# A decoder step on one core: the first two units run side by side on inputs that come in pieces of 256 KB, with zeros multiplied before and between

## The chip, the cores and the metric

The kernel runs on 1 core of one Trainium2 chip. The time is that of one execution on the device in microseconds (us); lower is better. Before the change the median of 3 runs is 2367.28 us (2366.43 to 2371.67).

## What is computed

One inference step of a decoder with two layers: 1024 prompt tokens and 8 single decode tokens, model width 2048, all in float32. Layer A mixes by pooling, layer B by attention over a sliding window:

```python
z = x @ w_in                               # 2048 -> 4096
u, gate = z[..., :D_POOL], z[..., D_POOL:]
d, new_state = multiscale_pool(u, prefix, pos)        # windows 2, 4, 8, 16 on four channel groups
d = jnp.einsum('btgc,gce->btge', d.reshape(B, T, 4, 512), w_grp)
y = (d.reshape(B, T, D_POOL) * scale * jax.nn.silu(gate)) @ w_out
x = layer_norm(ALPHA * x + y, g_ln, b_ln)
```

Then keys and values are projected once, and layer B does its query and gate projection, attention, output projection and norm. The change lies in the first 2% of the time: in `z = x @ w_in` for the first of the four channel groups.

## The kernel before

**Numbers in two parts.** A float32 operand is split into a high part (rounded to the matmul's type fp32r by a cast on ScalarE) and a low part (operand minus high part, on VectorE). A product is then three matmuls: high x high, high x low, low x high. So each weight block and each block of x costs one cast and one subtraction before its first full use.

**Units.** The tokens are cut in two chunks. The first stage, layer A's input projection of chunk 0 for channel group 0, is done plainly; later stages use a scheme with seven products for eight, whose operands are sums made on the way. A plain unit (`unit`, L648 on) makes 128 output channels for 512 tokens in one PSUM bank: two halves (`par`), each with one weight block (128 x 1024 numbers, 512 KB) and four blocks of x (each two of the 128-channel slices, 512 KB), eight slices of three matmuls (L669, L670, L671), 48 matmuls of 512 columns in all. The group has four such units for u, then four for the gate, and then the group's own product (`group_half`, L1071). Two neighbouring units use the same blocks of x, so x is split once and kept.

**The order of the work.** All of it is written out by Python in one order, and `in_order` keeps that order on TensorE, VectorE and ScalarE. A stream lists the weight blocks in the order of use. `begin` loads ahead (5 blocks), casts ahead (4) and makes low parts ahead (3) in plain stages, then hands out the next pair of high and low parts; `prep_to` (L489) emits the low parts, `cast_to` (L474) the casts, `load_to` (L273) the loads on SP. `end` closes a half of a half unit: it counts `i` up, runs the events due at `i`, and emits one of the sums that wait in `late`. `flush` emits what waits for a finished PSUM bank.

For the plain stage the four blocks of two neighbouring weight tiles (a and d of the first, b and c of the second) are also summed in four ways (`plain_pair`, `add1`, L279) and stored to DRAM by POOL for the second chunk; these sums are the `late` ones. `t_first` (L719 to L722) makes four blocks of sums from two blocks of x for the next stage, at events 3, 6, 9 and 12. A finished unit is copied from PSUM by ScalarE (L1132) and pooled on VectorE (`pool_tile`, L1017, L1025, L1028) at an event one step later.

**The start** (`start`, L2048 on). SP loads weight block a, four blocks of x, block d, two of x, block b, two of x, the small tables prm, cst, mki, and goes on with weights (c first). Eight DMAs of SP's queue can be under way: the ninth waits for the first, and so on. ScalarE casts and VectorE subtracts whole blocks (128 x 1024) in the order a, x 0 to 3, d, x 4 to 7; then nsink (L2077), a small scaling of a part of prm. Memory is 53 slots of 128 x 1040 numbers; a new tile takes the slot that has been free longest.

Of the kernel before, what the change touches and what calls it, by code (L numbers as in the profile page):

```python
# [16 lines left out]
P = 128  # L17
# [13 lines left out]
TP = 512  # L31
# [30 lines left out]
ORDERL = (0, 5, 2, 1, 3, 4, 6)  # L62
ENGINES = (mybir.EngineType.PE, mybir.EngineType.DVE, mybir.EngineType.Activation)
NSLOT = 53
KEEP0 = 1

SPLIT = 5, 6, 7
# [114 lines left out]
class Kern:  # L182
    def __init__(self, ctx, tc, io):
# [18 lines left out]
        self.sgd = [one.tile([P, 8, NDEC], F32, name=f"sgd{i}") for i in range(2)]  # L202
        self.mem = Mem(pool("mem", bufs=1), NSLOT)
        self.n = 0
# [62 lines left out]
        u, v = w[2 * q], w[2 * q + 1]  # L267
        return u[:, :1024], u[:, 1024:], v[:, :1024], v[:, 1024:]

    def load1(self, s, k, src):  # L270
        def go():
            s[k] = self.mem.full()
            self.nc.sync.dma_start(s[k].a[:, :1024], src)  # L273

        return go

# [9 lines left out]
    def plain_pair(self, name, q):  # L286

        a11, a12, a21, a22 = self.quads(name, q)
        ws = self.ws[name][q]
        s = {}  # L290
        ent = lambda k, src, after: Entry([self.load1(s, k, src)], [], lambda: s[k], after)
        late = [
            self.add1(s, "c", "b", "c", ws[:, 1, :]),
            self.add1(s, "b", "a", "b", ws[:, 0, :], "b"),
            self.add1(s, "a", "a", "c", ws[:, 2, :], "c"),
            self.add1(s, "d", "a", "d", ws[:, 3, :], "a", "d"),
        ]
        return [
            ent("a", a11, []),
            ent("d", a12, []),  # L300
            ent("b", a21, []),
            ent("c", a22, [lambda: self.late.extend(late)]),
        ]

    def lone(self, src):
        s = {}
        return Entry([self.load1(s, "a", src)], [], lambda: s["a"], [lambda: s.pop("a").free()])
# [347 lines left out]
    def unit(self, done):  # L655
# [3 lines left out]
        for par in range(2):  # L659
            w = self.begin()  # L660
            wh, wl = (s.r for s in w)
            for k in range(8):
# [16 lines left out]
                if k in (3, 7):  # L679
                    self.end()  # L680


    def x_begin(self, n):

        kind, c, part = PHASES[n]
        self.ready((INPUT_OF[kind], c, PHASES[n] in PLAIN))
        self.xkey, self.need = (INPUT_OF[kind], c), {}
        self.xseven = PHASES[n] not in PLAIN
        order = ORDERL if (kind, c) in LOCKED else ORDER7
        self.xq = [(i, g) for i in order for g in range(2)] if self.xseven else [  # L690
            (q, j) for q in range(2) for j in range(4)
        ]
        self.xraw, self.pre = self.pre, {}
        self.held = set(self.xraw)
        self.xhi, self.xnew = {}, {}
        if PHASES[n - 1] in PLAIN and PHASES[n - 1][:2] == (kind, c):

            T = CHUNKS[c][1]
            left = {s: 2 for j in range(4) for s in self.X[1, j]}
            self.shared = True  # L700
            for g in range(2):
                tiles = list(zip(self.X[1, 2 * g], self.X[1, 2 * g + 1]))
                for i, cs in ((5, slice(0, T // 2)), (4, slice(T // 2, T))):
                    self.xnew[i, g] = tuple(View(t, T, cs, left) for t in tiles)
            self.xq = [k for k in self.xq if k not in self.xnew]
        self.xl = [k for k in self.xq if k not in self.held]
# [408 lines left out]
    def phase_ai(self, c, gs, nxt):  # L1115
        nc, io = self.nc, self.io
        T = CHUNKS[c][1]
        TH = T // 2
        silu = lambda dst, ps: nc.scalar.activation(dst, ps, AF.Silu)
        for g in gs:  # L1120
            ext = es = None
            if T > TP:
                es = self.mem.half()
                ext = es.a[:, :512].rearrange("p (i b w) -> p i b w", i=4, b=NDEC)
                nc.sync.dma_start(ext, io["st"][:, 4 * g : 4 * g + 4])
            dd, sg = {}, {}
            for i in range(4):
                if not self.strassen:

                    def done(ps, i=i):  # L1130
                        U = self.mem.full()
                        nc.scalar.copy(U.a[:, NST : NST + T], ps[:])  # L1132
                        self.at(1, lambda: self.pool_tile(c, 4 * g + i, U, None, dd))

                    self.unit(done)
                elif i % 2 == 0:
                    us = {}

                    def z(j, us=us):
                        def go():  # L1140
                            us[j] = self.mem.full()
                            return us[j].a[:, NST : NST + T]

                        return go

                    def done(i=i, us=us):
                        n = i // 2
                        self.at(n, lambda: self.pool_tile(c, 4 * g + i, us[0], ext, dd))
                        self.at(n + 4, lambda: self.pool_tile(c, 4 * g + i + 1, us[1], ext, dd))

                    self.pair(c, z(0), z(1), done)
            if ext is not None:

                def put(es=es, ext=ext, g=g):
                    nc.sync.dma_start(io["nps"][:, 4 * g : 4 * g + 4], ext)
                    es.free()

                self.at(8, put)
            for i in range(4):
                if g == gs[-1] and i == 0:  # L1160
                    self.x_begin(nxt)
                if not self.strassen:

                    def done(ps, i=i):
                        if i % 2 == 0:
                            sg[i // 2] = self.mem.full()
                        silu(sg[i // 2].a[:, (i % 2) * T : (i % 2 + 1) * T], ps[:])

                    self.last = g == gs[-1] and i == 3
                    self.unit(done)  # L1170
                elif i % 2 == 0:
# [78 lines left out]
    def shifted(self, c, p, s, pre, acc, end):  # L1250
# [10 lines left out]
        def less():  # L1261
            t = self.pair_view(s, T)
            nc.vector.tensor_sub(t, t, self.l_sh[c].a[:, None, :T].to_broadcast([P, 2, T]))
            if p >= KEEP0:
                nc.gpsimd.dma_start(self.act["p", c][:, 2 * p : 2 * p + 2, :], t)
# [5 lines left out]
        def add():  # L1271
# [4 lines left out]
            box["q"].free()  # L1276
            if p >= KEEP0:
                s.free(True)
# [774 lines left out]
    def start(self):  # L2053
        nc, io = self.nc, self.io
        self.xkey, self.xseven = ("x", 0), False
        self.X, self.xnew, self.xraw, self.xhi = {}, {}, {}, {}
        self.xq = [(q, j) for q in range(2) for j in range(4)]
        self.xl = list(self.xq)
        self.x0, self.pre, self.held = {}, {}, set()
        self.load_to(1)  # L2060
        for n in range(8):
            self.x_load()
            if n in (3, 5):
                self.load_to(n // 2 + 1)
        nc.sync.dma_start(self.prm[:], io["prm"])
        nc.sync.dma_start(self.cst[:], io["cst"])
        nc.sync.dma_start(self.mki[:], io["mki"])
        self.prep_to(1)
        for n in range(8):
            self.x_make()  # L2070
            if n == 3:
                self.prep_to(2)
        for j in range(4):
            self.at(3 + 3 * j, lambda j=j: self.t_first(j))
        self.at(13, lambda: setattr(self, "x0", None))
        self.at(9, lambda: nc.scalar.copy(self.jr[:], self.cst[:, K_J : K_J + P]))
        nc.vector.tensor_scalar(  # L2077
            self.nsink[:], self.prm[:, C_SINK : C_SINK + NH], -1.0, None, op0=ALU.mult
        )
# [231 lines left out]
```

## Time and profile before

| what | value |
|---|---|
| median of 3 runs | 2367.28 us (2366.43 to 2371.67) |
| the profiled execution | 2367.62 us |
| its span (first to last instruction) | 2365.9 us |
| mean granted clock of TensorE | 0.996 |
| VectorE, ScalarE, POOL busy | 81%, 57%, 9% |
| data moved by DMA | 669.18 MB, 283 GB/s on average |
| DMA, 0 to 8 us, 8 to 13.3 us, 13.3 to 22 us | 242, 407, 399 GB/s |
| DMA, 34 to 100 us | 214 GB/s |

How to read it: the profile is of one execution. PE is TensorE's matmul, PEld its weight loads, DVE is VectorE, ACT ScalarE, POOL GpSimd, SP the engine that issues loads. A row of the timeline has the start in us, the duration in us, engine, line, operation, the tile written and the tile read (m is any of the memory slots, pD a PSUM bank), shapes, count, and in brackets the idle time before it with what ended it. A row of waits has who waited for whom, the sum in us, the number of times and the longest. A row of windows has, behind the stretch, its length, then busy us and count for PE, PEld, DVE, ACT and POOL, then the granted clock, the DMA engines' share and GB/s. A row of groups has busy us and mean ns of one behind the bar. Matmuls are pipelined: the start of one to the start of the next is what one costs, not its duration.

### The profile page before, as it was taken

Reading aid. Unit: us, or ns where it says so; the run is one execution under the profiler, and the core shown is the slowest. Engines: PE = TensorE matmul, PEld = TensorE weight load, DVE = VectorE, ACT = ScalarE, POOL = GpSimd, SP = SyncE. Lnnn points to the kernel's source line nnn. Section 1 sums busy time; section 2 is a strip of 40 time slices with the busy share of each in tenths; the row PEclk is TensorE's granted clock in tenths of the full one; section 3 lists DMA queues with packets and bytes.
Section 4 is the critical chain, followed back from the end, with each engine's and each line's share of the span. In section 5 each row is a group of like instructions: output and inputs, shape, how many; then the busy total and the mean of one; then the engine's idle time right before and its main releaser. Section 6 shows DMA issues by size and latency. Waiting matters only on the chain. (4 is left out here: it accounts for less than half of the span.)

```text
span 2365.9 us, 46542 instructions
## 1 busy us (share of the span) xinstructions
PE 2326.4 (98%) x18424; PEld 2219.4 (94%) x18424; DVE 1923.5 (81%) x2385; ACT 1342.2 (57%) x2429; POOL 201.5 (9%) x379
## 2 busy tenths in 40 slices
PE   8999999999999999999999999999999999999997
PEld 6899999999999999998778899999999999999997
DVE  8787998776878878868888888887777768888887
ACT  4444446544536547554554656685666667546556
POOL 0111110001000000000111111100000000000000
PEclk9999999999999999999999999999999999999999
DMA  8678789889889989989888766788787768699785
GB/s 294 215 244 303 274 291 349 308 308 315 286 278 365 331 270 324 334 314 330 282 324 322 258 230 224 238 297 275 232 259 221 222 193 298 227 353 371 259 302 194
DMA packets 252059, 669.18 MB, mean 283 GB/s; under 512 B 25760, under 2 KB 106560, under 8 KB 251840
## 3 DMA queue, kind: packets, MB, share of 16 engines
q1 hardware_dynamic: 206368, 501.14, 64.0%
q0 software_dynamic: 45472, 165.07, 17.9%
q8 instruction: 144, 2.36, 0.4%
q14 instruction: 75, 0.61, 0.1%
HBM read 471.01 MB, written 185.59 MB: 278 GB/s over the span
## 5 line engine op out<-in xcount | busy, mean ns | idle before, releaser
L641 PE MATMUL pD<-m,m 128*128 128x260 f32 (+1 forms) x4752 | 1346.9, 283 | 9.9 <-DVE m L602 3.7
L643 PE MATMUL pD<-m,m 128*128 128x260 f32 (+1 forms) x4752 | 1340.5, 282 | 4.5 <-DVE m L489 4.5
L642 PE MATMUL pD<-m,m 128*128 128x260 f32 (+1 forms) x4752 | 1340.3, 282 | 0.0
L641 PEld LDWEIGHTS pD<-m,m 128*128 128x128 f32 x4752 | 896.0, 189 | 21.0 <-issue 10.2
L643 PEld LDWEIGHTS pD<-m,m 128*128 128x128 f32 x4752 | 896.7, 189 | 6.0 <-DVE m L489 6.0
L642 PEld LDWEIGHTS pD<-m,m 128*128 128x128 f32 x4752 | 896.3, 189 | 0.5
L489 DVE TENSOR_TENSOR m<-m,m 128x1024 fp32r<-128x1024 f32 x674 | 814.1, 1219 | 96.1 <-ACT m L474 58.3
L474 ACT CAST m<-m 128x1024 fp32r<-128x1024 f32 x674 | 701.6, 1048 | 305.2 <-DVE m L332 71.3
L669 PE MATMUL pD<-m,m 128*128 128x512 f32 x448 | 179.7, 401 | 8.0 <-ACT m L752 8.0
L670 PE MATMUL pD<-m,m 128*128 128x512 f32 x448 | 177.2, 396 | 0.5 <-DVE m L761 0.5
L671 PE MATMUL pD<-m,m 128*128 128x512 f32 x448 | 177.2, 396 | 0.0
L761 DVE TENSOR_TENSOR m<-m,m 128x1024 fp32r<-128x1024 f32 (+1 forms) x120 | 146.9, 1225 | 7.2 <-ACT m L752 5.7
L614 ACT COPY m<-pD 128x260 f32<-128x260 f32 (+1 forms) x83 | 31.0, 373 | 188.2 <-PE pD L643 188.1
L752 ACT CAST m<-m 128x1024 fp32r<-128x1024 f32 (+1 forms) x120 | 125.7, 1052 | 14.2 <-PE pD L670 5.2
L669 PEld LDWEIGHTS pD<-m,m 128*128 128x128 f32 x448 | 84.7, 189 | 29.9 <-ACT m L752 8.0
L332 DVE TENSOR_TENSOR m<-m,m 128x1024 f32<-128x1024 f32 x88 | 107.6, 1222 | 5.9 <-DMA m<-in_wia 4.2
L670 PEld LDWEIGHTS pD<-m,m 128*128 128x128 f32 x448 | 84.8, 189 | 20.4 <-DVE m L761 1.6
L671 PEld LDWEIGHTS pD<-m,m 128*128 128x128 f32 x448 | 84.6, 189 | 19.8
L602 DVE TENSOR_TENSOR m<-pD,m 128x260 f32<-128x260 f32 (+1 forms) x86 | 36.4, 424 | 81.9 <-PE pD L643 78.6
L1778 ACT ACTIVATE m<-m,sm 128x128 f32<-128x128 f32 x256 | 99.2, 390 | 0.0
L1071 PE MATMUL pD<-m,m 128*128 128x260 f32 (+1 forms) x528 | 91.5, 323 | 0.0
L607 DVE TENSOR_TENSOR m<-pD,m 128x260 f32<-128x260 f32 (+1 forms) x84 | 35.6, 424 | 64.2 <-PE pD L643 64.0
(243 smaller groups left out, 2167.3 us busy)
## 6 DMA issues: line engine op xcount, KB each, us to landing
m<-in_wia SPq DMA_DIRECT2D x124, 512.0 KB
m<-in_wib SPq DMA_DIRECT2D x120, 512.0 KB
swia<-m POOLq DMA_DIRECT2D x64, 512.0 KB, 4.9
m<-swia SPq DMA_DIRECT2D x64, 512.0 KB
m<-swoa SPq DMA_DIRECT2D x64, 512.0 KB
swib<-m POOLq DMA_DIRECT2D x64, 512.0 KB, 5.3
m<-swib SPq DMA_DIRECT2D x64, 512.0 KB
m<-swob SPq DMA_DIRECT2D x56, 512.0 KB
```

The lines of the kernel that those rows point to most:

```text
L332: self.nc.vector.tensor_add(s[out].a[:, :1024], s[x].a[:, :1024], s[y].a[:, :1024])
L474: self.nc.scalar.copy(hi.r[:, :1024], self.stream[self.cast].src().a[:, :1024])
L489: self.nc.vector.tensor_sub(lo.r[:, :1024], s.src().a[:, :1024], hi.a[:, :1024])
L641: nc.tensor.matmul(ps[:, :TH], wh[:, s], h, start=new and k == 0, stop=False, skip_group_check=on)
L642: nc.tensor.matmul(ps[:, :TH], wh[:, s], l, start=False, stop=False, skip_group_check=on)
L643: nc.tensor.matmul(ps[:, :TH], wl[:, s], h, start=False, stop=k == 7, skip_group_check=on)
L669: nc.tensor.matmul(ps[:], wh[:, s], h, start=par == 0 and k == 0, stop=False)
L670: nc.tensor.matmul(ps[:], wh[:, s], l, start=False, stop=False)
L671: nc.tensor.matmul(ps[:], wl[:, s], h, start=False, stop=par == 1 and k == 7)
L752: self.nc.scalar.copy(h.r[:, :n], s.a[:, :n])
L761: self.nc.vector.tensor_sub(l.r[:, :n], s.a[:, :n], h.a[:, :n])
L1778: nc.scalar.activation(x["s3"][:, i, :], x["s3"][:, i, :], AF.Exp, bias=nm[:, i : i + 1], scale=0.125, accum_out=rs[:, i : i + 1],)
```

## The change

The first two units run side by side. `first_units` takes the place of the first two calls of `unit`: for each block of x it does six matmuls of the first unit and then six of the second, into two PSUM banks. The first pair's stream is a, b, d, c instead of a, d, b, c.

`start` loads the first half (512 columns, 256 KB) of a, both slices of x block 0 apart (256 KB each), the first half of b, both slices of x block 1, the second half of a, x block 2, the second half of b, x block 3, then d, x 4, c, x 5, x 6, x 7, one weight block more, and prm, cst, mki. Casts and subtractions follow the same pieces, in the same order.

A tile of zeros is made by VectorE, and 17 matmuls of it (256 columns, into a bank of its own) come before the first real one; four stand behind the first real matmul, one in the second slice, and one behind each of the first three groups of six.

Both finished units are handed to ScalarE together; the pooling of the second comes at an event three steps later instead of one. In the built program, VectorE's order behind the last subtraction of x is now nsink, four sums (add1), four operations of t_first, the low part of the third unit's first weights; before it was nsink, the low parts of b and c, two sums, t_first, that low part, and then the other two sums. After the third unit's start TensorE's instructions are the same, in the same order, in both programs; the slots that tiles get differ.

```diff
+WARM = 17
+FILL = 4, 1, 1, 1, 1
...
-        return [
+        e = [
             ent("a", a11, []),
             ent("d", a12, []),
             ent("b", a21, []),
             ent("c", a22, [lambda: self.late.extend(late)]),
         ]
+        return [e[0], e[2], e[1], e[3]] if first else e
...
+    def idle(self, n):
+        z = self.zero
+        for _ in range(n):
+            self.nc.tensor.matmul(self.zps[:, :256], z.r[:, :P], z.r[:, P:384], start=True, stop=True)
+
+    def first_units(self, dones):
+        nc = self.nc
+        banks = [self.psD() for _ in dones]
+        for par in range(2):
+            ws = {}
+            for n, (u, j) in enumerate((u, j) for j in range(4) for u in range(2)):
+                if u not in ws:
+                    ws[u] = self.begin()
+                elif n % 2 == 0:
+                    self.flush()
+                wh, wl = (a.r for a in ws[u])
+                x = self.x_get((par, j))
+                for i in range(2):
+                    k = 2 * j + i
+                    s = slice(k * P, (k + 1) * P)
+                    h, l = (a.rv(2, TP)[:, i, :] for a in x)
+                    nc.tensor.matmul(banks[u][:], wh[:, s], h, start=par == 0 and k == 0, stop=False)
+                    if par == 0 and n == 0:
+                        self.idle(FILL[i])
+                    nc.tensor.matmul(banks[u][:], wh[:, s], l, start=False, stop=False)
+                    nc.tensor.matmul(banks[u][:], wl[:, s], h, start=False, stop=par == 1 and k == 7)
+                if par == 0 and n < 3:
+                    self.idle(FILL[2 + n])
...
+                        n = 3 if g == 0 and i == 1 else 1
+                        self.at(n, lambda: self.pool_tile(c, 4 * g + i, U, None, dd))
+                    if c == 0 and g == 0 and i < 2:
+                        twins.append(done)
+                        if i == 1:
+                            self.first_units(twins)
+                    else:
+                        self.unit(done)
...
-        self.load_to(1)
-        for n in range(8):
+        z = self.zero = self.mem.full()
+        nc.vector.memset(z.a[:, :384], 0.0)
+        self.zps = self.psD()
+        self.idle(WARM)
...
+        plan = [
+            ("a", 0, 512), ("x", 0, TP), ("x", TP, 2 * TP), ("b", 0, 512), ("y", 0, TP), ("y", TP, 2 * TP),
+            ("a", 512, 1024), None, ("b", 512, 1024), None,
+        ]
...
+            nc.scalar.copy(h.r[:, lo:hi], raw[k].a[:, lo:hi])
+            nc.vector.tensor_sub(l.r[:, lo:hi], raw[k].a[:, lo:hi], h.a[:, lo:hi])
```

In the changed file the lines of the same operations are L282 (sums), L481 and L496 (cast and low part of weights), L676 to L678 (matmuls of `unit`), L712, L715, L716 (matmuls of `first_units`), L693 (zeros), L768 to L771 (t_first), L801 and L810 (cast and low part of x), L1182 (copy from PSUM), L2163 and L2164 (cast and low part of a half piece).

More of the change, by code (lines that the diff above doesn't have):

```diff
@@ L268, in quads, with load1 @@
         return u[:, :1024], u[:, 1024:], v[:, :1024], v[:, 1024:]
-    def load1(self, s, k, src):
+    def load1(self, s, k, src, cuts=((0, 1024),)):
         def go():
             s[k] = self.mem.full()
-            self.nc.sync.dma_start(s[k].a[:, :1024], src)
+            for a, b in cuts:
+                self.nc.sync.dma_start(s[k].a[:, a:b], src[:, a:b])
         return go
@@ L290, in plain_pair @@
         s = {}
+        first = name == "wia" and q == 0
+        if first:
+            self.first_w = s
         ent = lambda k, src, after: Entry([self.load1(s, k, src)], [], lambda: s[k], after)
@@ L679, in unit @@
                 if k in (3, 7):
+                    self.end()
+    def idle(self, n):
[25 more added lines that the diff above has]
+                    self.idle(FILL[2 + n])
+                if par == 0 and n == 3:
+                    self.zero.free()
+                if u == 1:
+                    self.x_used((par, j))
+                if n == 7:
+                    for w in ws.values():
+                        for a in w:
+                            a.free()
+                    if par == 1:
+                        self.posts += [lambda ps=ps, done=done: done(ps) for ps, done in zip(banks, dones)]
+                if n % 2:
                     self.end()
@@ L1126, in phase_ai @@
             dd, sg = {}, {}
+            twins = []
             for i in range(4):
@@ L1132, in done @@
                         nc.scalar.copy(U.a[:, NST : NST + T], ps[:])
-                        self.at(1, lambda: self.pool_tile(c, 4 * g + i, U, None, dd))
-                    self.unit(done)
+                        n = 3 if g == 0 and i == 1 else 1
[6 more added lines that the diff above has]
+                        self.unit(done)
                 elif i % 2 == 0:
@@ L2059, in start @@
         self.x0, self.pre, self.held = {}, {}, set()
-        self.load_to(1)
-        for n in range(8):
+        z = self.zero = self.mem.full()
+        nc.vector.memset(z.a[:, :384], 0.0)
+        self.zps = self.psD()
+        self.idle(WARM)
+        qa, _, qb, _ = self.quads("wia", 0)
+        src = [self.act["x", 0][:, 4 * j : 4 * j + 4 : 2, :] for j in range(2)]
+        raw = {k: self.mem.full() for k in "abxy"}
+        both = {k: (self.mem.full(), self.mem.full()) for k in "abxy"}
+        plan = [
+            ("a", 0, 512), ("x", 0, TP), ("x", TP, 2 * TP), ("b", 0, 512), ("y", 0, TP), ("y", TP, 2 * TP),
+            ("a", 512, 1024), None, ("b", 512, 1024), None,
+        ]
+        for it in plan:
+            if it is None:
+                self.xl = [k for k in self.xq[2:] if k not in self.xraw]
+                self.x_load()
+                continue
+            k, lo, hi = it
+            if k in "ab":
+                nc.sync.dma_start(raw[k].a[:, lo:hi], {"a": qa, "b": qb}[k][:, lo:hi])
+            else:
+                nc.sync.dma_start(raw[k].a[:, lo:hi], src["xy".index(k)][:, lo // TP, :])
+        for e in self.stream[:2]:
+            e.loads[0] = lambda: None
+        self.load_to(2)
+        for n in range(4, 8):
+            if n in (4, 5):
+                self.load_to(n - 1)
             self.x_load()
-            if n in (3, 5):
-                self.load_to(n // 2 + 1)
+        self.load_to(5)
         nc.sync.dma_start(self.prm[:], io["prm"])
@@ L2067, in start @@
         nc.sync.dma_start(self.mki[:], io["mki"])
-        self.prep_to(1)
-        for n in range(8):
+        self.first_w.update(a=raw["a"], b=raw["b"])
+        self.hl[0], self.hl[1] = both["a"], both["b"]
+        self.cast = self.made = self.prepped = 2
+        for n, k in enumerate("xy"):
+            self.x0[0, n], self.xnew[0, n] = raw[k], both[k]
+        self.xq = self.xq[2:]
+        for it in plan:
+            if it is None:
+                self.x_make()
+                continue
+            k, lo, hi = it
+            h, l = both[k]
+            nc.scalar.copy(h.r[:, lo:hi], raw[k].a[:, lo:hi])
+            nc.vector.tensor_sub(l.r[:, lo:hi], raw[k].a[:, lo:hi], h.a[:, lo:hi])
+        for n in range(4, 8):
+            if n in (4, 5):
+                self.prep_to(n - 1)
             self.x_make()
-            if n == 3:
-                self.prep_to(2)
         for j in range(4):
```

## The prediction

> **What bounds the kernel now.** I read the page first, for the share of the engines.
>
> ```profile
> span 2365.9 us, 46542 instructions
> PE 2326.4 (98%) x18424; PEld 2219.4 (94%) x18424; DVE 1923.5 (81%) x2385; ACT 1342.2 (57%) x2429; POOL 201.5 (9%) x379
> ```
>
> TensorE is idle for 2365.9 - 2326.4 = 39.5 us in all, so whatever does not shorten its work can bring only a part of these. The table of TensorE's waits says where they lie.
>
> ```profile
> PE pD L669 <- ACT m L752: 8.0, 1, 8.0
> PE pD L643 <- DVE m L489: 4.5, 7, 1.4
> PE pD L641 <- ACT pD L582: 3.6, 4, 1.9
> PE pD L670 <- DVE m L761: 0.5, 1, 0.5
> ```
>
> The longest single wait is the start. The change touches only the first two units (96 matmuls of 512 columns), so next I read the timeline of the first 34 us, where SP's loads, ScalarE's casts (high parts), VectorE's subtractions (low parts) and the matmuls stand beside each other.
>
> ```profile
> 5.20 1.04 ACT L474 CAST m<-m 128x1024 fp32r<-128x1024 f32 x1 [3.19 <-DMA m<-in_wia]
> 6.86 1.04 ACT L752 CAST m<-m 128x1024 fp32r<-128x1024 f32 x1 [0.61 <-DMA m<-in_x]
> 7.93 1.22 DVE L761 TENSOR_TENSOR m<-m,m 128x1024 fp32r<-128x1024 f32 x1 [0.43 <-ACT m L752]
> 7.96 0.79 PE L669 MATMUL pD<-m,m 128*128 128x512 f32 x1 [7.96 <-ACT m L752]
> 9.21 0.80 PE L670 MATMUL pD<-m,m 128*128 128x512 f32 x1 [0.47 <-DVE m L761]
> ...
> 12.79 0.61 PE L669 MATMUL pD<-m,m 128*128 128x512 f32 x1
> 13.22 0.41 PE L670 MATMUL pD<-m,m 128*128 128x512 f32 x1
> 13.47 0.39 PE L671 MATMUL pD<-m,m 128*128 128x512 f32 x1
> 13.70 0.39 PE L669 MATMUL pD<-m,m 128*128 128x512 f32 x1
> ...
> 18.72 1.05 ACT L752 CAST m<-m 128x1024 fp32r<-128x1024 f32 x1 [0.35 <-DMA m<-in_x]
> 19.80 1.23 DVE L761 TENSOR_TENSOR m<-m,m 128x1024 fp32r<-128x1024 f32 x1 [0.18 <-ACT m L752]
> 21.00 1.06 ACT L474 CAST m<-m 128x1024 fp32r<-128x1024 f32 x1 [0.28 <-DMA m<-in_wia]
> ```
>
> The first matmul starts at 7.96, the second at 9.21. They then follow 0.43 us apart (12.79 to 13.22) until 13.2, and 0.23 us apart from 13.47 on: TensorE runs at half speed until 5.3 us after its first matmul. A cast starts right as its load lands: the first 512 KB at 5.20, the second at 6.86, the eleventh at 18.72, so (18.72 - 6.86) / 9 = 1.32 us for each 512 KB. Matmuls follow without a gap by the time the second unit ends:
>
> ```profile
> 33.44 0.39 PE L669 MATMUL pD<-m,m 128*128 128x512 f32 x1
> 33.66 0.40 PE L670 MATMUL pD<-m,m 128*128 128x512 f32 x1
> 33.90 0.40 PE L671 MATMUL pD<-m,m 128*128 128x512 f32 x1
> ```
>
> These are matmuls 97 to 99, the first three of the third unit. From the first, (33.44 - 13.70) / 84 = 0.235, and without the two short waits near 20 us 0.231 us each. Matmul 99 at 33.90 is my mark: it is the first that needs the low part of the third unit's first weights, and from there on both programs issue the same matmuls.
>
> **The change part by part: the first 96 matmuls.** Loads. The first 256 KB land, by half of the 1.66 us between the first two loads, at about 4.4 (between 3.9, a whole 1.32 us earlier, and 5.2); the first half of x then at 5.2. For half pieces I take these rows of 512 columns:
>
> ```profile
> L261 ACT CAST m<-m 128x512 fp32r<-128x512 f32 x1 | 0.6, 625 | 7.8 <-DVE m L1028 7.8
> 25.82 0.69 DVE L719 TENSOR_TENSOR m<-m 128x512 f32<-128x512 f32 x1
> 26.42 0.69 DVE L720 TENSOR_TENSOR m<-m,m 128x512 f32<-128x512 f32 x1
> 27.02 0.69 DVE L721 TENSOR_TENSOR m<-m,m 128x512 f32<-128x512 f32 x1
> 27.75 0.69 DVE L722 TENSOR_TENSOR m<-m,m 128x512 f32<-128x512 f32 x1
> 28.36 1.22 DVE L489 TENSOR_TENSOR m<-m,m 128x1024 fp32r<-128x1024 f32 x1
> 29.49 2.48 DVE L279 TENSOR_TENSOR m<-m,m 128x1024 f32<-128x1024 f32 x2
> 31.89 0.68 DVE L1017 TENSOR_TENSOR m<-m 128x512 f32<-128x512 f32 x1
> ```
>
> A half cast takes 0.62, so the first real matmul starts at 5.2 + 0.62 + 0.06 = 5.9 (2.1 earlier than 7.96). Low parts follow 0.60 to 0.69 apart: weights 5.0 to 5.7, x 5.85 to 6.55, so the second matmul starts at 6.6 (2.6 earlier). Until matmul 25, six half pieces pass VectorE (the last low part near 9.6), while 24 matmuls take 24 x 0.231 = 5.55 us; the waits that are left, and the zeros in them, add 1.0 by my count. So matmul 25 starts at 5.9 + 5.55 + 1.0 = 12.4. From there a whole piece of x (1.32 us) feeds twelve matmuls (2.78 us), and 72 x 0.231 brings matmul 97 to 29.1, against 33.44. TensorE would gain 4.3 us.
>
> Zeros. The 17 are multiplied once VectorE's memset is through (under 0.7 us after 0.74, so from 1.4). For 256 columns I take the windows around the one later place where the clock fell:
>
> ```profile
> 360.00:364.00 4.00, 3.26 (x18) 3.26 (x19) 3.97 (x4) 3.87 (x6) 0.53 (x1) 0.68 1.03 340
> 372.00:376.00 4.00, 4.00 (x37) 4.00 (x36) 3.86 (x5) 2.44 (x3) 0.00 (x0) 1.00 1.04 393
> ```
>
> At full clock a matmul of 256 columns takes 4.00 / 37 = 0.11 us; slow, twice that, 0.22. Seventeen take 3.7 us, to 5.1: nothing is late through them. The four zeros behind the first real matmul take 0.45 to 0.9 where a wait of 0.5 stands anyway, the other four 0.11 to 0.22 each; at worst 0.9 in all. The clock is free between 1.4 + 4.0 = 5.4 (counting as from the second matmul of before, 9.21 to 13.2) and 1.4 + 5.3 = 6.7, so at most two or three real matmuls are slow, 0.2 us each.
>
> The Trainium skill, TensorE: Matmul & The Clock Gate, section "What's actually happening", speaks against counting on 17 zeros: its window of about 3.4 us runs free, so the release can come up to two windows after the first matmul. By it the clock would be free between 4.8 and 8.2, and matmul 97 would come at most 1.1 later, at 30.2; the 5.3 us of the trace lies inside that span. The sum below would stay, for the next part decides.
>
> **VectorE's order behind the pieces.** Here the gain is cut. In the built order, VectorE now has, after the last low part of x: nsink, all four sums of the first weights (L279), the four operations of t_first (L719 to L722), and only then the low part for the third unit (L489). Before, only two of the sums stood ahead of it (28.36, the other two at 29.49). And the last piece of x is now the twelfth 512 KB in the queue, not the eleventh, since the weights c go ahead of it: it lands at 18.72 + 1.32 = 20.04. Its low part starts 1.08 later, as at 19.80 above: 21.12. With nsink it takes 1.23 (19.80 to the next start at 21.03):
>
> ```profile
> 21.03 2.35 DVE L489 TENSOR_TENSOR m<-m,m 128x1024 fp32r<-128x1024 f32 x2
> 23.42 2.48 DVE L279 TENSOR_TENSOR m<-m,m 128x1024 f32<-128x1024 f32 x2
> ```
>
> The sums start at 22.35; two took 23.42 to 25.82 = 2.40, four in a chain 3 x 1.25 + 1.15 = 4.9: 27.25. The four operations of t_first took 25.82 to 28.36 = 2.54: 29.79. The low part takes 1.22: 31.01, and matmul 99 starts at 31.07. TensorE wanted it at 29.1 + 0.46 = 29.5, so a new wait of 1.5 us on L489 stands there; behind it TensorE has only the rest of that unit, and ScalarE's copy of that unit's bank is the first to wait for it, 11 us on. The gain is 33.90 - 31.07 = **2.8 us**. Behind it nothing is late: the next low part ends near 32.2 and is wanted at 31.07 + 22 x 0.231 = 36.2, the one after (behind another t_first, 2.54) at 35.8 for 41.7.
>
> The rest costs nothing. The two PSUM banks are copied by ScalarE after 29.1 instead of one at 23.18 and one at 34.06; ScalarE is busy 57%. The pooled tile of the second unit goes two steps later, and needs nothing before the group's product. The stores of the sums go out on POOL about 4 us earlier, beside loads that have slack then (214 GB/s from 34 to 100 us). prm, cst and mki move behind one more load on SP; nsink could wait if prm landed after 22.2, but the three together took only 21.00 - 18.72 - 1.32 = 0.96 us. Memory slots are numbered otherwise afterwards, with the same matmuls in the same order; I take nothing for it, and 4.5 us either way as its bound (the later stall of 1.9 us on L582, 4.00 - 3.26 = 0.7 more beside it and 18 slow matmuls, 18 x 0.1).
>
> The profiled run took 2367.62 us, 1.7 over its span, and 0.3 over the median 2367.28. From the median: 2367.28 - 2.8 = **2364.5 us**.
>
> **The rivals.**
> - *TensorE alone sets the third unit* (pieces land earlier, or VectorE packs tighter): the whole 4.3, 2363.0. For it: VectorE has no DMA to wait for once the pieces are there. Against it: the chain of 9.95 us from 21.12 is made of durations that hardly vary.
> - *The zeros do not raise the clock*, so the change does not do what it says. Then real matmuls are slow from 5.9 to 5.9 + 5.3 = 11.2, ten or so with their zeros; matmul 97 comes near 31.3, and 99 at 31.8: 2.1 gained, 2365.2.
> - *The new wait lowers the clock.* The 1.9 us wait on L582 and 0.7 more (4.00 - 3.26) stood at the row with clock 0.68; one wait of 1.5 is shorter. The price is that row's 18 slow matmuls, 0.1 each: 1.8 lost, 2366.3.
> - *A DMA of 256 KB costs as much as one of 512 KB* (slower than before). Eight half pieces would each take up to 0.66 more, the last x lands 5.3 later, and matmul 99 starts at 36.4: 2.5 lost, 2369.8. It decides from (33.90 - 31.07) / 8 = 0.35 us a piece on. Against it: prm, cst and mki, three DMAs, cost 0.32 each in all. The Trainium skill, DMA: Bandwidth & Descriptors, section "Bandwidth", asks for 1 MiB or more per DMA for three quarters of the peak; the 512 KB of this trace, several in flight, run at 0.524 / 1.32 = 397 GB/s, so here the measurement speaks against it.
>
> **How the numbers follow.** Forecast 0.55; TensorE alone 0.17; slow zeros 0.08; clock lowered 0.08; costly pieces 0.07; 0.05 for a later stall that comes or goes (2360 or 2369). The likeliest gives 2364.5. The range holds the forecast with an error of 1 us in the landing of the last x (it passes one to one), TensorE alone with 1 us more, slow zeros and lowered clock, and stops short of costly pieces: 2361.5 to 2368.5. 0.2% is 4.7 us, about what a measurement of this kernel can tell from no change. Below 2362.5 lie a third of "TensorE alone", a tenth of the forecast and half of the later stall: 0.15 to 0.17. Above 2372.0 lies little: 0.05. Between them 0.78.
>
> **What would show it.** First matmul of L712 near 5.9 and spaced 0.23 by 7; matmul 25 near 12.4; the last x cast at 20.0; four L282 at 22.35; L496 for the third unit from 29.8 to 31.0, with one TensorE wait of about 1.5 us on it, at L678. If that wait is absent and the third unit starts at 29.1, the chain is wrong and the gain is 4.3. If the first x is cast after 6, the pieces are costlier than half.

## The result, and the profile after

| | before | after |
|---|---|---|
| median of 17 runs each | 2368.02 us (2366.32 to 2371.69) | 2372.46 us (2370.44 to 2375.09) |
| the profiled execution, its span | 2367.62, 2365.9 us | 2372.92, 2371.2 us |
| TensorE's mean clock | 0.996 | 0.995 |

The ratio after to before is 1.0018, with a 95% interval of 1.0011 to 1.0025. The kernel became 4.4 us slower; forecast were 2.8 us faster and a range that ended at 2368.5. The page's row of engines and TensorE's waits after (who waits for whom, us in all, times, longest) already say that something new stands somewhere:

```profile
PE 2329.3 (98%) x18449; PEld 2223.4 (94%) x18449; DVE 1924.4 (81%) x2390; ACT 1343.1 (57%) x2433; POOL 202.1 (9%) x379
```

```profile
PE pD L650 <- DVE m L496: 11.1, 7, 7.5
...
PE pD L678 <- DVE m L496: 1.2, 1, 1.2
```

The wait of 8.0 us at the start is gone (1.11 is left at L712, in the timeline below), and the forecast wait at L678 is there with 1.2. But the waits of L650 (L643 before) grew from 4.5 to 11.1 in the same seven places: one of them lasts 7.5 us. So there are two questions, the start and that wait.

**The start.** The timeline after, from 0 to 36 us:

```profile
1.32 3.56 PE L693 MATMUL pD<-m 128*128 128x256 f32 x17 [1.32 <-DVE m L2117]
6.00 0.51 PE L712 MATMUL pD<-m,m 128*128 128x512 f32 x1 [1.11 <-ACT m L2163]
6.34 0.63 PE L693 MATMUL pD<-m 128*128 128x256 f32 x4
6.81 0.41 PE L715 MATMUL pD<-m,m 128*128 128x512 f32 x1
12.65 0.40 PE L712 MATMUL pD<-m,m 128*128 128x512 f32 x1
13.67 0.50 PE L715 MATMUL pD<-m,m 128*128 128x512 f32 x1 [0.62 <-DVE m L810]
21.05 1.05 ACT L801 CAST m<-m 128x1024 fp32r<-128x1024 f32 x1 [0.20 <-DMA m<-in_x]
23.36 5.00 DVE L282 TENSOR_TENSOR m<-m,m 128x1024 f32<-128x1024 f32 x4
30.25 0.40 PE L676 MATMUL pD<-m,m 128*128 128x512 f32 x1
30.81 2.35 DVE L496 TENSOR_TENSOR m<-m,m 128x1024 fp32r<-128x1024 f32 x2
32.09 0.50 PE L678 MATMUL pD<-m,m 128*128 128x512 f32 x1 [1.21 <-DVE m L496]
```

The 17 zeros, the first real matmul at 6.00, matmul 25 at 12.65, the last cast of x at 21.05, four sums, the low part, and the third unit's matmuls 97 (30.25) and 99 (32.09) stand in the order foretold. Matmul 99 comes 33.90 - 32.09 = 1.81 us earlier than before.

**The loss.** That lead is lost near 2130 us, far from the edit. TensorE's windows there, after and then before:

```profile
2100.00:2150.00 50.00, 42.51 (x350) 42.30 (x349) 36.48 (x51) 20.65 (x29) 4.25 (x8) 0.93 0.96 350
2150.00:2200.00 50.00, 49.10 (x412) 48.72 (x411) 45.76 (x44) 37.23 (x48) 1.06 (x2) 1.00 0.94 340
```

```profile
2100.00:2150.00 50.00, 50.00 (x426) 50.00 (x426) 40.66 (x56) 22.53 (x30) 4.25 (x8) 1.00 1.00 367
2150.00:2200.00 50.00, 47.43 (x390) 46.58 (x390) 46.39 (x44) 38.01 (x49) 1.06 (x2) 1.00 0.98 360
```

Before, TensorE had no idle time from 2100 to 2150. After, it is idle for 50.00 - 42.51 = 7.49 us, and the granted clock has a mean of 0.93 in that window: the trace's record has 0.50 from 2137.53 to 2144.36. From matmul 99 on both programs issue the same matmuls, so each can be set beside its twin. This is the one that waits (after, then before):

```profile
2141.42 0.58 PE L650 MATMUL pD<-m,m 128*128 128x256 f32 x1 [7.49 <-DVE m L496]
```

```profile
2134.92 0.28 PE L643 MATMUL pD<-m,m 128*128 128x256 f32 x1
```

The matmul ahead of it came 1.15 us earlier than before, this one comes 6.50 later, and the slow ones that follow until 2144.36 (0.21 us apart, not 0.12) bring that to 7.9: a swing of about 9 us on TensorE. Two stores by POOL, one on each side of the place, show the same for VectorE, which they follow (after, then before):

```profile
2121.17 0.53 POOL L862 DMA_DIRECT2D to<-m  x1 [6.63 <-DVE m L861]
2143.14 0.53 POOL L1321 DMA_DIRECT2D p<-m  x1 [3.11 <-DVE m L1319]
```

```profile
2122.41 0.53 POOL L813 DMA_DIRECT2D to<-m  x1 [6.63 <-DVE m L812]
2136.42 0.53 POOL L1265 DMA_DIRECT2D p<-m  x1 [3.11 <-DVE m L1263]
```

Of the lead of 1.81 us, 2122.41 - 2121.17 = 1.24 is left at the first store; at the second, the kernel is 2143.14 - 2136.42 = 6.72 behind. The swing there is 7.96 us, 7.76 of it one wait of VectorE (next). From 2150 to 2200 TensorE is busy for 49.10 us instead of 47.43: before has waits there that after has no more. Matmul for matmul after is 5.4 behind at 2200, and the spans end 2371.2 - 2365.9 = 5.3 apart.

What TensorE waits for is a low part, and VectorE in its turn (rows after, then before) waits for a load:

```profile
2137.52 0.43 DVE L858 TENSOR_TENSOR m<-m 128x260 f32<-128x260 f32 x1 [7.76 <-DMA m<-o]
2140.15 1.22 DVE L496 TENSOR_TENSOR m<-m,m 128x1024 fp32r<-128x1024 f32 x1
```

```profile
2130.81 0.42 DVE L809 TENSOR_TENSOR m<-m 128x260 f32<-128x260 f32 x1
```

A subtraction (L858, L809 before) reads a block of o, an intermediate in DRAM. Before, the block is there; after, VectorE stands for 7.76 us, and the low part that TensorE wants stands behind it in VectorE's fixed order. SP's queue, after and then before, shows why:

```profile
2115.90 0.32 SPq L871 DMA_DIRECT2D m<-o  x1
2118.18 0.33 SPq L276 DMA_DIRECT2D m<-in_wob  x1
2119.48 2.77 SPq L276 DMA_DIRECT2D m<-swob  x2
2128.18 0.33 SPq L276 DMA_DIRECT2D m<-in_wob  x1
2128.61 0.38 SPq L1260 DMA_DIRECT2D m<-h  x1
2129.08 0.38 SPq L871 DMA_DIRECT2D m<-o  x1
```

```profile
2117.14 3.01 SPq L822 DMA_DIRECT2D m<-o  x2
2120.32 0.33 SPq L273 DMA_DIRECT2D m<-in_wob  x1
2120.75 2.73 SPq L273 DMA_DIRECT2D m<-swob  x2
2125.17 0.32 SPq L1204 DMA_DIRECT2D m<-h  x1
2131.74 0.33 SPq L273 DMA_DIRECT2D m<-in_wob  x1
```

Before, the two last loads of o go out together, the second by 2120.2. After, the second stands behind four weight loads and one of h in the same queue. The last of those weight loads goes out at 2128.18, about 6 us behind the one ahead of it, and o at 2129.08: 9 us later than before. SP's waits from 2115 to 2130 say what held that weight load:

```profile
SPq L276 <- DMA to<-m: 5.9, 1, 5.9
```

It waits for a store by POOL out of a memory slot; that this is the slot which the load is to fill is inferred. The load of o is read 8.4 us after its issue (2137.52). Before, SP also had a weight load that came late (2131.74, after a like wait of 6.2), but this load of o was not behind it.

No line of the diff names o. What the diff does alter is which memory slots are free when: a new tile takes the slot that has been free longest, and the first units take and give back their slots in another order. So 2000 us on, the same tile lies in another slot. `in_order` fixes TensorE, VectorE and ScalarE, not SP; in the built program SP's loads stand in another order. The theory: **the start gains 1.8 us, and the new place of one load of o in SP's queue, which comes from the slots alone, costs 8 to 9 us there.** The rivals: something in the first units themselves costs the time (zeros, small pieces), or any other numbering of the slots would do the same.

### The profile page after: what moved, and what is told of

Read it like the earlier page. It is cut to its first block, busy times and chain, and to the rows that moved or that the text cites. A ratio compares the mean times of both kernels' runs of the same rounds, so it can differ in the third digit from the quotient of the medians.

```text
span 2371.2 us, 46617 instructions
## 1 busy us (share of the span) xinstructions
PE 2329.3 (98%) x18449; PEld 2223.4 (94%) x18449; DVE 1924.4 (81%) x2390; ACT 1343.1 (57%) x2433; POOL 202.1 (9%) x379
## 5 line engine op out<-in xcount | busy, mean ns | idle before, releaser
L650 PE MATMUL pD<-m,m 128*128 128x260 f32 (+1 forms) x4752 | 1341.6, 282 | 11.1 <-DVE m L496 11.1
L650 PEld LDWEIGHTS pD<-m,m 128*128 128x128 f32 x4752 | 897.9, 189 | 12.6 <-DVE m L496 12.6
L496 DVE TENSOR_TENSOR m<-m,m 128x1024 fp32r<-128x1024 f32 x672 | 812.2, 1220 | 92.0 <-ACT m L481 50.5
L481 ACT CAST m<-m 128x1024 fp32r<-128x1024 f32 x672 | 699.5, 1048 | 298.0 <-DVE m L339 71.2
L676 PE MATMUL pD<-m,m 128*128 128x512 f32 x416 | 165.9, 399 | 0.0
L678 PE MATMUL pD<-m,m 128*128 128x512 f32 x416 | 163.8, 394 | 1.2 <-DVE m L496 1.2
L677 PE MATMUL pD<-m,m 128*128 128x512 f32 x416 | 163.8, 394 | 0.0
L810 DVE TENSOR_TENSOR m<-m,m 128x1024 fp32r<-128x1024 f32 (+1 forms) x118 | 144.6, 1227 | 3.6 <-ACT m L801 2.0
L801 ACT CAST m<-m 128x1024 fp32r<-128x1024 f32 (+1 forms) x118 | 123.7, 1052 | 12.9 <-PE pD L677 5.2
L676 PEld LDWEIGHTS pD<-m,m 128*128 128x128 f32 x416 | 78.2, 188 | 20.4 <-issue 3.2
L678 PEld LDWEIGHTS pD<-m,m 128*128 128x128 f32 x416 | 78.2, 188 | 19.8 <-DVE m L496 1.6
```

Of the source, the lines that this page charges most:

```text
L481: self.nc.scalar.copy(hi.r[:, :1024], self.stream[self.cast].src().a[:, :1024])
L496: self.nc.vector.tensor_sub(lo.r[:, :1024], s.src().a[:, :1024], hi.a[:, :1024])
L650: nc.tensor.matmul(ps[:, :TH], wl[:, s], h, start=False, stop=k == 7, skip_group_check=on)
L676: nc.tensor.matmul(ps[:], wh[:, s], h, start=par == 0 and k == 0, stop=False)
L677: nc.tensor.matmul(ps[:], wh[:, s], l, start=False, stop=False)
L678: nc.tensor.matmul(ps[:], wl[:, s], h, start=False, stop=par == 1 and k == 7)
```

## The experiments

### after_turn: the changed kernel with other slots

One line moves the slot that has been free longest to the end of the list, once, at event 8. No instruction of any engine is added or taken away; with it the last two loads of o stand together on SP again.

```diff
+    def turn(self):
+        i = min(self.whole(), key=lambda i: max(self.f[i]))
+        self.clock += 1
+        self.f[i] = [self.clock, self.clock]
...
+        for k in (8,):
+            self.at(k, self.mem.turn)
```

> The changed kernel, with one free memory slot moved once to the back of the line of free slots (at event 8, no instruction of its own): in the built program the second-last load of attention output o for the transform then stands on SP ahead of the weight loads again, as before the change. Theory A (the late load): the 7.5 us wait of TensorE on a low part near 2132 us and the slow clock behind it go, matmul 99 still starts at 32.1 (1.8 ahead of before), and of these 1.8 about 1.2 are left by 2100 us as in the changed kernel's trace: 2366.2 to 2366.8, some 6 us below the changed kernel. Rival B (the new start itself shifts the phases against each other, whatever slot is used): the wait stays, about 2372.5.

Measured: median 2365.32 us of 11 runs (2364.02 to 2368.25), before 2368.01; ratio 0.9992 (0.9983 to 1.0001). The profiled run took 2365.32. SP's row, and matmul 99:

```profile
2114.93 4.73 SPq L876 DMA_DIRECT2D m<-o  x2
```

```profile
32.16 0.50 PE L683 MATMUL pD<-m,m 128*128 128x512 f32 x1 [0.36 <-DVE m L501]
```

Both loads of o go out by 2119.7, TensorE has no wait from 2100 to 2150, and 7.1 us are gone from the median of after. Matmul 99 starts as in after (32.16 against 32.09), so the first units are not what costs the time. The median lies 0.9 below the range expected, and its interval still reaches 1. In this trace one stretch of slow clock near 360 us is missing, 3.4 us at 0.50 in the traces of before and after; the lead over before grows from 1.6 at 350 us to 3.1 at 400. Seven of the twelve traces of this case have that stretch and five don't, so a single trace can stand 1.5 us off for this alone.

### before_turn: the kernel before with other slots

The same edit on the kernel before, at event 12, where it puts the second load of o late. The first units are as before.

```diff
+        for k in (12,):
+            self.at(k, self.mem.turn)
```

> The kernel before, its start untouched, with one free slot moved once to the back of the line (at event 12): in the built program the same load of o then stands behind two weight loads, as in the changed kernel. Theory A: a TensorE wait of about 7.5 us on a low part near 2133 us, 1.7 us of slow clock behind it, less about 3 us of smaller waits that it takes the place of: 2373 to 2375. Rival B: no such wait, 2368.

Measured: median 2377.63 us of 5 runs (2373.39 to 2381.06); ratio 1.0043 (1.0029 to 1.0056). The waits of the profiled run (2373.39 us) from 2100 to 2150, and SP's second load of o:

```profile
DVE m L814 <- DMA m<-o: 6.2, 1, 6.2
...
PE pD L648 <- DVE m L494: 5.9, 1, 5.9
```

```profile
2128.87 0.38 SPq L827 DMA_DIRECT2D m<-o  x1
```

The kernel before, without the change, gets the stall by slots alone. In the profiled run TensorE goes from 0.2 us ahead of before to 8.1 behind, and 5.4 are left at 2200 us, as in after. The median is 4 us higher than this run and above the range expected. Why is open: the other four runs have no trace. Their mean granted clock is 0.994 to 0.995, against 0.996 in the profiled run; since 0.001 of 2371 us is 2.4 us, more slow stretches could make up much of it.

### other_turn: a control

The changed kernel with the slots turned at event 16 instead of 8; here the load of o stays late.

```diff
-        for k in (8,):
+        for k in (16,):
```

> A control for e1: the changed kernel with a free slot turned once, but at event 16, after which the built program still has the load of o behind two weight loads on SP. If the place of that load is the cause, the wait near 2132 us stays (5 us or more on one low part) and the time is about 2372. If turning slots helps for another reason, 2366.

Measured: median 2373.31 us of 9 runs (2371.28 to 2376.23), before 2367.53; ratio 1.0025 (1.0015 to 1.0034). The waits from 2100 to 2150:

```profile
DVE m L863 <- DMA m<-o: 7.3, 1, 7.3
...
PE pD L655 <- DVE m L501: 7.0, 1, 7.0
```

Turning a slot as such is no cure: where o stays late, the stall stays. Nor does any other order of the loads do the same: read by the tensors that SP loads, its queue differs from before's in a dozen or more places behind the start, in each of these versions. The swap near 2120 us stands in after, before_turn and other_turn, which stall, and not in after_turn or, below, in sums_later, which don't.

### o_on_pool: the slots as they are, o on another queue

The changed kernel with its own slots; only the loads of o for the transform are issued by POOL.

```diff
-            self.nc.sync.dma_start(s[kp].v(2, T), self.act[key][:, 2 * kp : 2 * kp + 2, :])
+            q = self.nc.gpsimd if key == ("o", 1) else self.nc.sync
+            q.dma_start(s[kp].v(2, T), self.act[key][:, 2 * kp : 2 * kp + 2, :])
```

> The changed kernel, slots as they are, with only the eight loads of o for the transform issued by POOL instead of SP, so that none of them stands behind a weight load. If it is the place of the last of them on SP that costs, it is issued some 6 us earlier (behind the store that POOL issues at 2121), VectorE does not wait 7.8 us for it, TensorE's wait of 7.5 us goes, and the time is 2366 to 2367. If the load is late for another reason (its slot, or the DMA rate), the wait stays and the time is about 2372.

Measured: median 2366.93 us of 10 runs (2365.05 to 2370.94), before 2367.61; ratio 0.9998 (0.9989 to 1.0007). The load of o and its reader:

```profile
2123.70 0.55 POOL L872 DMA_DIRECT2D m<-o  x1 [4.04 <-issue]
2129.14 0.43 DVE L858 TENSOR_TENSOR m<-m 128x260 f32<-128x260 f32 x1 [1.43 <-DMA m<-o]
```

The load goes out 5.4 us earlier than in after (2.0 of this because the whole run is that much ahead there) and is read 5.4 us after its issue instead of 8.4; VectorE's wait falls from 7.76 to 1.43, TensorE's from 7.5 to 1.2. This separates the place in SP's queue from all else that the slots alter: with after's slots unchanged, 5.5 us of its median are gone.

### no_zeros: what the zeros are worth

after_turn without the multiplied zeros; nothing reads their product.

```diff
-WARM = 17
-FILL = 4, 1, 1, 1, 1
+WARM = 0
+FILL = 0, 0, 0, 0, 0
```

> e1 without the matmuls of zeros (none ahead, none in the gaps). If VectorE's chain sets matmul 99, it stays at 32.1 to 32.4 although real matmuls are slow from 6.0 to about 11.3 (each 0.2 us longer), and the time is that of e1 within 0.3 us. If the zeros carry the gain, matmul 99 starts at 33 or later and the time is 1 us or more above e1.

Measured: median 2365.65 us of 10 runs (2363.99 to 2369.85); ratio 0.9993 (0.9984 to 1.0002). The first real matmul starts at 6.69, and the matmuls stay 0.43 us apart until 12.28. Yet:

```profile
32.25 0.40 PE L683 MATMUL pD<-m,m 128*128 128x512 f32 x1
```

Matmul 99 comes only 0.1 later than in after_turn and 0.16 later than in after. It has no wait here: without zeros TensorE itself sets it, 0.2 us behind the end of the low part (30.81 + 1.22). With the clock free early, TensorE reaches matmul 97 at 30.25 (after) instead of 31.79, but then has to wait for that low part, so VectorE's chain takes nearly all that the zeros give. Here they buy nothing that the medians show (2365.32 and 2365.65).

### whole_pieces, weights_whole, x_whole: what the small pieces are worth

after_turn with every block whole (512 KB); then with the weights alone whole, and with x alone whole (one run each).

```diff
         plan = [
-            ("a", 0, 512), ("x", 0, TP), ("x", TP, 2 * TP), ("b", 0, 512), ("y", 0, TP), ("y", TP, 2 * TP),
-            ("a", 512, 1024), None, ("b", 512, 1024), None,
+            ("a", 0, 1024), ("x", 0, 2 * TP), ("b", 0, 1024), ("y", 0, 2 * TP), None, None,
```

> e1 with the first two weight blocks and the first two blocks of x loaded, cast and subtracted whole (512 KB each). If the pieces of 256 KB leave too few bytes under way (eight DMAs at a time; the DMA rate fell to about 245 GB/s between 6.8 and 9 us), the dip goes and the last block of x is cast at 20.0 instead of 21.05, and the third unit's first low part ends at 31.0 instead of 32.0. The first real matmul comes at 7.9 instead of 6.0. If the pieces have nothing to do with it, the last x is cast at 21.05 still and matmul 99 is at 32 or later.

Measured: median 2367.54 us of 10 runs (2365.44 to 2368.68); ratio 0.9997 (0.9988 to 1.0006). Its timeline:

```profile
8.41 0.50 PE L717 MATMUL pD<-m,m 128*128 128x512 f32 x1 [3.09 <-ACT m L2167]
...
20.26 1.05 ACT L806 CAST m<-m 128x1024 fp32r<-128x1024 f32 x1 [0.20 <-DMA m<-in_x]
...
33.61 0.40 PE L681 MATMUL pD<-m,m 128*128 128x512 f32 x1
```

With whole blocks the first matmul comes 2.4 later than after's 6.00 and the third unit at 33.61; TensorE is now the late one, by 34.07 - 32.16 = 1.9 us at matmul 99, and the medians differ by 2.2. Matmul 99 is no earlier than before (33.90): without the small pieces the new order gains nothing. The zeros don't help here: the trace has full speed from 5.81 us, but behind the wait of 3.09 the granted clock is 0.50 from 9.22 to 12.63. But the last x is cast at 20.26, 0.8 *earlier* than after's 21.05. So the small pieces do cost something. Which ones:

> e1 with the first two weight blocks whole (512 KB) and only x in halves. What cost the 1.0 us by which the last x landed later than forecast: if it is the halves of the weights, the last x is cast at 20.0 to 20.3 as with whole pieces (20.26 in e4); if it is the halves of x, at 21.0.

> e1 with the first two blocks of x whole and only the weights in halves. If the halves of the weights are dear, the last x is cast at 21.0; if those of x, at 20.0 to 20.3.

The last cast of x, with the weights whole, and then with x whole:

```profile
21.20 1.06 ACT L806 CAST m<-m 128x1024 fp32r<-128x1024 f32 x1 [0.21 <-DMA m<-in_x]
```

```profile
20.33 1.05 ACT L806 CAST m<-m 128x1024 fp32r<-128x1024 f32 x1 [0.20 <-DMA m<-in_x]
```

One run each took 2368.09 and 2368.58 us. Whole weights bring no earlier x (21.20); whole x brings it to 20.33. The other traces give the scatter: in the eight with x in halves the last cast of x comes at 20.74 to 21.20, 21.0 on average, in the two with x whole at 20.26 and 20.33. It is the four halves of x that cost about 0.7 us; the halves of the weights show no cost above a scatter of 0.4. Why a half of x costs more than a half of the weights stays open.

### sums_later: the sums out of the way

after_turn with the first pair's four sums parted again: two stay ahead of the third unit's low part, two go behind it, as they stood before the change (turns at events 8 and 9 keep the loads of o together).

```diff
-            ent("c", a22, [lambda: self.late.extend(late)]),
+            ent("c", a22, [lambda: self.sums_late(late, first)]),
...
+    def sums_late(self, late, first):
+        k = 2 if first else 4
+        self.late.extend(late[:k])
+        if first:
+            self.at(4, lambda: self.late.extend(late[k:]))
```

> e1 with two of the four sums of the first weights put behind the third unit's low part on VectorE (as before the change), and with the free slots turned so that the load of o stays early. If VectorE's chain sets matmul 99, the low part starts two sums (2.45 us) earlier, near 28.4, and TensorE runs through: matmul 99 at 30.7 to 31.7 (by how soon the clock is free in the profiled run) instead of 32.1, the time 0.5 to 1.4 us below e1: 2363.9 to 2364.8. If something else holds matmul 99, it stays at 32.1 and the time at 2365.3.

Measured: median 2363.59 us of 11 runs (2362.13 to 2365.43), before 2367.53; ratio 0.9983 (0.9974 to 0.9992).

```profile
28.16 2.35 DVE L507 TENSOR_TENSOR m<-m,m 128x1024 fp32r<-128x1024 f32 x2
30.09 0.40 PE L687 MATMUL pD<-m,m 128*128 128x512 f32 x1
...
30.55 0.40 PE L689 MATMUL pD<-m,m 128*128 128x512 f32 x1
```

The low part starts at 28.16 instead of 30.81, and matmul 99 follows 97 without a wait, at 30.55: 3.35 us earlier than before. This version is faster than both kernels, and alone among the runs its interval lies wholly below 1.

### sums_no_zeros: the zeros, where TensorE is the late one

sums_later without the zeros, whose product nothing reads. Its diff is that of no_zeros.

> e5 without the matmuls of zeros. In e5 TensorE itself sets matmul 99 (30.55, no wait), so here the slow clock must show, unlike in e3: real matmuls slow until about 12, matmul 99 at 31.8 to 32.3, the time 1.2 to 1.7 us above e5: 2364.8 to 2365.3. If the zeros are worth nothing here either, 2363.6.

Measured: median 2364.91 us of 11 runs (2363.49 to 2367.64), before 2367.61; ratio 0.9991 (0.9982 to 1.0).

```profile
31.06 0.40 PE L689 MATMUL pD<-m,m 128*128 128x512 f32 x1
```

Matmul 99 is 0.5 us later than with zeros. Where TensorE sets the third unit, the zeros are worth that much in this pair of traces; I had expected more, but the first real matmul came at 5.70 here (5.97 in sums_later, 6.69 in no_zeros). It hangs on how soon the clock is free, which differs between runs (last section): in after_turn, where it was free late, TensorE reached matmul 97 at 31.18, later than here without zeros (30.60). The medians, each against the before of its own chip, are 3.9 and 2.7 below it, with intervals that overlap.

## Why the prediction was wrong

**The step that failed** is one sentence of mine: "Memory slots are numbered otherwise afterwards, with the same matmuls in the same order; I take nothing for it, and 4.5 us either way as its bound". The same matmuls in the same order do not make the same program: SP's queue is not among what is kept in order. The swing at one place was 7.96 us on VectorE and about 9 on TensorE, not 0, and 6.5 of it stayed (from 1.15 ahead to 5.4 behind). This lies outside the bound, which I had taken from one later stall in the trace of before (1.9 us and its slow matmuls near 360 us). That was neither the longest nor the only one: its waits also have 2.6 us on L1778, and its granted clock is 0.83 from 1360 to 1370 us. In any case, a stall that isn't there yet isn't bounded by those that are. The case had its place among the rivals ("a later stall that comes or goes", 0.05, 2369), with too small a chance and too small a price. after_turn, before_turn and o_on_pool together show the cause: the slots alone bring it to the kernel before, and the queue alone takes most of it from the kernel after.

The rest, by its steps:

- *The first matmuls.* Right: 6.00 for 5.9, the second at 6.81 for 6.6, 0.23 apart from there, matmul 25 at 12.65 for 12.4.
- *Zeros and clock.* The zeros do raise the clock, as forecast, but the time was partly luck: in after it was free at 4.20, sooner than the forecast 5.4 to 6.7 (the four zeros at 6.34 take 0.12 each), in after_turn only at 9.97, later than the forecast and than the 8.2 that the prediction had as the latest (below). The rival of a new wait that lowers the clock did not come true: the wait of 1.21 at matmul 99 left it at 1.00.
- *TensorE at the third unit.* 30.25 for 29.1. Of the 1.15, 0.25 stood at matmul 25 already, and 1.02 instead of 0.23 passed between matmuls 25 and 26 (12.65 to 13.67), the second of which waited for a low part of x: there I had said that x would be ahead.
- *The last x.* The mis-sized term: cast at 21.05 for 20.04. I gave the halves nothing here; whole pieces give 20.26, and halves of x make the difference. My rival of costly pieces had up to 0.66 for each of eight; about 0.2 for each of four was measured.
- *VectorE's order.* Right: sums at 23.36 (22.35 + 1.0), low part at 30.81 (29.8 + 1.0), one wait at L678, 1.21 for 1.5. So the gain at matmul 99 was 1.81 for 2.8, and the missing 1.0 is the last x. sums_later confirms it from the other side: without two of the sums, the wait is gone.
- *What is kept of a gain.* I took the 2.8 as a gain of the whole run. Of the 1.81, 1.24 was left at 2121 us; what took the 0.6 on the way stays open.

With both terms as measured at the stores, the sum is 2367.62 - 1.24 + 7.96 = 2374.3. The profiled run ended at 2372.92; the 1.4 between are what the later waits gave back (6.72 behind at the second store, 5.3 at the end). This is a tally of one pair of traces, not a check of it.

## What to carry to other kernels

Where tiles take whatever buffer is free, an edit at the start can change the order of loads anywhere behind it: compare the loading engine's queue over the whole program, not only the engines whose order is fixed, and look for loads that slip behind one that waits for its buffer, above all where the DMA engines' share is near 1.00 and one load takes 8 us. Such a loss says nothing on the edit itself, and turning one buffer, or giving the load a queue of its own, parts the two. Keeping TensorE warm paid where TensorE was the late one, 0.5 us in one pair of traces (sums_later), and 0.1 to 0.2 behind VectorE's chain.

## What the runs showed of the hardware that was not expected

- *The clock's release varies between runs with the same start.* The 17 zeros start at 1.32 in all runs that have them. The traces' record of the granted clock begins with the release (a row of windows shows 1.00 ahead of that, where nothing is recorded): 4.20 us in after, 4.51 to 6.71 in six others, 9.97 in after_turn, so 2.9 to 8.6 us after the first zero. The rows agree: in after the zeros take 3.56 us and the matmuls are at full speed by 6.34; in after_turn the zeros take 3.99, and the matmuls stay 0.43 us apart until 9.96, across a gap of 0.85 us ahead of the first real matmul. Without zeros (no_zeros) it came 5.6 us after the first matmul (6.69 to 12.28). The Trainium skill, TensorE: Matmul & The Clock Gate, section "What's actually happening", has windows of about 3.4 us that run free, so a varying release agrees with it; 8.6 us is more than two such windows. Counted back from 9.97 in steps of 3.4, the gap (5.32 to 6.17) lies in one window of after_turn, while in after the release came ahead of the gap (1.11 us); that the gap cost after_turn a window fits both, but no run here tests it. These rows are after_turn's:

```profile
1.32 3.99 PE L698 MATMUL pD<-m 128*128 128x256 f32 x17 [1.32 <-DVE m L2122]
9.96 0.29 PE L698 MATMUL pD<-m 128*128 128x256 f32 x1
```

- *One idle stretch lowers the clock again*: 7.5 us near 2135 give 0.93 over the 50 us around it, where the kernel before has 1.00. At the start, waits of 1.73 to 3.09 us for the first real matmul (the three versions with whole pieces) were followed by 3.4 us at 0.50, one of 1.11 us (after) was not.
- *Halves of x and halves of weights aren't alike*: four DMAs of 256 KB in place of two of 512 KB delay the last load by about 0.7 us for x (21.0 on average against 20.3), and for weights by nothing above the scatter of 0.4.
